# Spatial mixing products for eight feature tiles at once, and earlier operands for two down projections

## The chip, the cores and the metric

The kernel runs on one core of one Trainium2 chip. The metric is device time in microseconds for one execution, the lower the better. Engines are named as in the profile: PE is TensorE (matrix products; PEld its weight loads), DVE is VectorE, ACT is ScalarE, POOL is GpSimd, SP is SyncE, which issues most of the DMA transfers.

## The reference

A two-layer trunk on `x` of 256 frames by 2048 features, all float32. Each sub-layer is `x <- LayerNorm(ALPHA * x + sublayer(x))`. Layer 0 mixes tokens with a gated spatial MLP, layer 1 with latent attention; each is followed by a gated MLP ("ffn") with a causal convolution of width 3. What the change touches is the spatial MLP and both ffn:

```python
def gmlp_mixer(x, w_in, ln_g, ln_b, w_s, b_s, w_out):
    z = jax.nn.gelu(x @ w_in)                 # 2048 -> 2 * 6144
    u, v = jnp.split(z, 2, axis=-1)
    v = layer_norm(v, ln_g, ln_b)
    v = v.reshape(B, S // 128, 128, 8, 768)   # windows of 128 frames, 8 groups of features
    w = w_s * mask[None]                      # 8 x 128 x 128
    s = jnp.einsum('gij,bnjgd->bnigd', w, v) + jnp.transpose(b_s)[None, None, :, :, None]
    return (u * s.reshape(B, S, 6144)) @ w_out

def conv_ffn(x, w_up, conv_w, conv_b, w_down):
    h = x @ w_up                              # 2048 -> 2 * 5504
    h = conv(h, conv_w) + conv_b              # width 3, causal, one filter a feature
    a, g = jnp.split(h, 2, axis=-1)
    return (jax.nn.silu(g) * a) @ w_down
```

## The kernel before

Every float32 operand is held as a high and a low part, and a product is made of high x high, low x high and high x low. Weights stream in chunks of 1 MB: `Feed` loads a chunk into one of three raw buffers (SP's queue), ACT casts its high part `wh` (L127), DVE subtracts to get the low part `wl` (L130). Both lie in a pool of 14 large buffers ("big"), which also holds activations and the operands of the down projections. PSUM has 8 banks of 128 x 512 float32, handed out as they come free.

The stages run one after the other. In layer 0: the `v` half of the up projection and its norm; then the `u` half, 12 groups (`gi`) of four feature tiles of 128 features by 256 frames, four weight chunks a group. In a group `prod_a` accumulates the four tiles in four banks: for each pair of chunks 32 products with `wh` (512 wide: the high and the low part of x side by side), then 32 with `wl` (256 wide) or the other way about. Behind the group, `gate` takes each tile F: `sum_halves` adds the bank's two halves (`lo_u` on ACT, L391; `h_u` on DVE, L393), ACT applies Gelu, PE makes two spatial products `s` of 128 x 128 in a bank of its own, DVE makes the bias term `sb` (L796), scales the two windows (`sg`, twice, L801) and multiplies (`pT`, L803). `v` must be normalised for them, which `norm_v` does for slice `gi // 2 + 1` within the even groups.

`down(NF_GM, pT, "wo")` then multiplies `pT` with the output weights, in two passes over pairs of feature tiles ("units") in the order of the table `PLAN`. A unit is "wide" (the three products above), "seven" (a scheme with seven products in place of eight, with sums of operands) or "parked" (the same, with weight sums computed beforehand, stored in DRAM by POOL's DMAs and fetched). Its accumulators stand in two sets of four banks, DIRECT and OWN; the first pass takes banks for DIRECT first. `acts.make` builds the high and low operands of a unit (`wo0wx`, `dn00wx`, `dn01px`: projection, unit, kind); L476 is the cast of a parked unit's turned sums, L479 and L480 the cast and the subtraction of the operand itself. `down` makes three units ahead of use; what is made earlier is done by the loops that feed it.

The ffn of a layer runs 22 groups; group 0 belongs to the boundary of the stages and groups 1 to 21 to its loop. A group is four tiles (two pairs `a`, `g`), each convolved (`conv`: L838 on ACT, L839 and L841 on DVE), then Silu (L855) and the product `act`. After group 19 the loop makes the operands of the first two units, after group 20 those of the third; then `down` follows. Layer 1's attention and its ffn use the same helpers. All products of PE are recorded under one line, L234. Instructions of an engine run in the order in which its queue holds them, which a scheduler decides from the program's order and its model of times; a weight cast of `Feed` can come ahead of an earlier evacuation and the reverse.

Of the kernel before, what the change touches and what calls it, by code (L numbers as in the profile page):

```python
# [8 lines left out]
F32 = mybir.dt.float32  # L9
F32R = mybir.dt.float32r  # L10
BF16 = mybir.dt.bfloat16
AF = mybir.ActivationFunctionType
# [48 lines left out]
        NF_FF: ("0e 1p 2e 3s 4e 5e 6p 7e 8s 9e 10e 11p 12e 13s 14e 15p 16e 17s 18e 19s 20e 21e",  # L61
                "21e 20e 19p 18e 17s 16e 15p 14e 13s 12e 11p 10s 9e 8s 7p 6e 5s 4e 3e 2e 1e 0e")}
KINDS = {"e": "wide", "s": "seven", "p": "parked"}
LEAD = 5
KEEP = {"wide": 4, "seven": 6, "parked": 6}

# [147 lines left out]
def trunk(ctx: ExitStack, tc: tile.TileContext, x, xT, gm_in, gm_wout, ffn_up, ffn_dn,  # L214
# [12 lines left out]
    def slot(shape, name, dt=F32, tag="big"):  # L227
        return big.tile(shape, dt, tag=tag, name=name, bufs=SLOTS[tag])

    def bank(name):  # L230
        return ps.tile([P, 512], F32, tag="bank", name=name)

    def mm(o, l, r, start, stop):
        recent[0] = nc.tensor.matmul(o, l, r, start=start, stop=stop, skip_group_check=True)  # L234
# [250 lines left out]
    def down(n_k, src, tag, ln, acts, skew=SKEW):  # L485

        ln.begin()
        seq = plan(n_k)
        line = seq[0] + seq[1]
        late, at = [], 0  # L490
        fetched = max([i for i, t in enumerate(line) if t[1] == "parked"], default=len(line))
        for hf, units in enumerate(seq):
            n = len(units)
            last = [u for u, kind in units if kind != "wide"][-1]
            acc = Banks(f"{tag}{hf}", OWN + DIRECT if hf else DIRECT + OWN)
            for i, (u, kind) in enumerate(units):
                left = n - 1 - i if hf == 1 else n
                for n2, v2 in enumerate(line[at : at + 3]):
                    acts.make(*v2, "side" if at + n2 > fetched or at + n2 >= len(seq[0]) and v2[1] == "parked" else "big")
                if i == n - 8:  # L500
                    ln.fetch(hf)
                got = feed.next(splits=2 if left > 5 or left == 0 else 3, loads=2 if left > 2 or left == 0 else 1)
                if left == 6:
                    ln.prep()
                a, sums = acts.got[u]
                if left < skew:
                    late.append((a, *got))
                elif kind == "wide":
                    acc.eight(a, *got)
                else:  # L510
                    acc.seven(a, sums, *got, 512 if kind == "parked" else 0)
                    if u == last:
                        for j, t in enumerate(acc.rest()):
                            ln.fold(j // 2, 2 * hf + j % 2, t)
                at += 1
                for v2 in [v2 for v2 in acts.got if not any(v2 == w2 and n2 < KEEP[kind2]
                                                            for n2, (w2, kind2) in enumerate(line[at:]))]:
                    acts.got.pop(v2)
            if hf == 0:
                for j, m in enumerate(DIRECT):  # L520
# [260 lines left out]
    pT = [None] * 6  # L781
    acts = Acts(pT, "wo", NF_GM)

    def gate(F, acc):
        g = F // 6
        sl, pos = F // 8, F % 8
        if pT[sl] is None:
            pT[sl] = slot([P, 8, S], f"pT{sl}", tag="side" if sl else "big")
        h = sum_halves(acc, f"u{F}")
        u = tp.tile([P, S], F32, tag="t1", name=f"u{F}", bufs=T1)  # L790
        nc.scalar.activation(u, h, AF.Gelu_apprx_tanh)
        sp = bank(f"s{F}")
        for b in range(2):
            mm(sp[:, b * P : (b + 1) * P], v[sl][:, b, pos * P : (pos + 1) * P], wTg[:, g, :], True, True)
        t = tp.tile([P, P], F32, tag="sbias", name=f"sb{F}", bufs=1)
        nc.vector.scalar_tensor_tensor(t, rowsum[:, g, :], cst[:, C_GMB + F : C_GMB + F + 1], bsb[:, g, :],  # L796
                                       ALU.mult, ALU.add)
        s = tp.tile([P, S], F32, tag="t1", name=f"sg{F}", bufs=T1)
        for b in range(2):
            c = slice(b * P, (b + 1) * P)  # L800
            nc.vector.scalar_tensor_tensor(s[:, c], sp[:, c], cst[:, C_GMG + F : C_GMG + F + 1], t,  # L801
                                           ALU.mult, ALU.add)
        nc.vector.tensor_tensor(pT[sl][:, pos, :], u, s, ALU.mult)  # L803

    def park_all(until):

# [5 lines left out]
    for gi in range(12):  # L812
        acc = [bank(f"u{gi}_{f}") for f in range(4)]
        for c in range(4):
            hi, lo = feed.next()
            prod_a(acc, xhl, range(4 * c, 4 * c + 4), hi, lo)
            if gi > 0:
                next(jobs, None)
            if gi % 2 == 0 and gi < 10 and c in (1, 2):
                norm_v(gi // 2 + 1, c - 1)  # L820
        if gi == 11:
            for t in plan(NF_GM)[0][:2]:
                acts.make(*t)
        for f in range(4):
            gate(4 * gi + f, acc[f])
        if gi == 10:
            acts.make(*plan(NF_GM)[0][2])

# [16 lines left out]
    def ffn(layer, ln, acc, end, last):  # L845
# [28 lines left out]
        for gi in range(1, 22):  # L874
            nt, nk = (4, 4) if gi < 21 else (2, 8)
            acc = [bank(f"up{layer}_{gi}_{f}") for f in range(nt)]
            for c in range(KD // nk):
                hi, lo = feed.next()
                prod_a(acc, xhl, range(nk * c, nk * c + nk), hi, lo)
                if gi > 1:  # L880
                    next(jobs, None)
                if gi == 1 and c == 0:
                    after(1, 1, None)
                    for f in range(2):
                        pair(f, hb[0][:, f * S : (f + 1) * S], hb[1][:, f * S : (f + 1) * S])
            for f in range(nt // 2):
                pair(2 * gi + f, acc[f], acc[nt // 2 + f])
            if 1 < gi < 6:
                old.restore(gi - 2)
            if gi in (4, 6):  # L890
                old.park(gi // 2 - 2)
            if gi == 19:
                for t in plan(NF_FF)[0][:2]:
                    acts.make(*t)
            if gi == 20:
                acts.make(*plan(NF_FF)[0][2])
        ln = Norm(2 * layer + 1, {}, old.put_away, last)
        return (ln, *down(NF_FF, act, f"dn{layer}", ln, acts, 4 if last else SKEW))

# [372 lines left out]
```

## Time and profile before

| | |
|---|---|
| Median of 3 runs | 2488.39 us (2487.24 to 2489.69) |
| Profiled execution | 2486.63 us, its span 2484.8 us |
| Mean granted PE clock | 0.999 |
| PE busy | 2468.0 us, 99% |
| DVE busy | 1992.9 us, 80% |
| ACT busy | 1424.6 us, 57% |
| DMA | 606.17 MB, mean 244 GB/s |

The span is what the profile covers; the execution's own time is 1.8 us longer. Busy shares are averages over all stages. The u groups lie between about 279 and 545 us of the span, the `wo` projection begins at 545; chunk 2 of the ffn's group 20 (chunk 226 of the whole stream) begins in layer 0 near 1262 us, its fellow in layer 1 near 2230 us.

### The profile page before, as it was taken

The page shows a single profiled execution, that of the slowest core. Times are in us where ns is not written, and L with a number is a line of the kernel's source. Part 1 is how long each engine was busy: PE and PEld are TensorE (multiplying, and loading weights), DVE is VectorE, ACT ScalarE, POOL GpSimd, SP SyncE. Part 2 cuts the span into 40 slices and gives each one's busy share as a digit, 9 for nine tenths or more (in the row PEclk, how much of TensorE's full clock was granted, in tenths as well). Part 3 has the DMA queues.
Part 4 walks back from the last instruction along what each step waited for, and adds up shares of the span by engine and source line. Part 5 has one row for each costly group of instructions (what it writes and reads, how often), then busy time and mean ns, then how long its engine had stood idle before and what let it go on. Part 6 is the DMA issues. An engine that isn't in the chain of part 4 may idle for free. (4 is left out here: it accounts for less than half of the span.)

```text
span 2484.8 us, 33520 instructions
## 1 busy us (share of the span) xinstructions
PE 2468.0 (99%) x12995; PEld 2122.3 (85%) x12995; DVE 1992.9 (80%) x2802; ACT 1424.6 (57%) x1979; POOL 89.0 (4%) x173
## 2 busy tenths in 40 slices
PE   9999999999999999999999999999999999999998
PEld 7888888888888888888888888988888888888886
DVE  7999866679898789787677897856598788768798
ACT  6676544446565756566554566655566656655453
POOL 0000000000000000000000000000001000000000
PEclk9999999999999999999999999999999999999999
DMA  7556544546665689788558885544489789647885
GB/s 280 203 206 223 198 173 169 185 170 214 209 203 203 218 349 351 286 335 315 188 198 319 302 305 185 182 155 151 174 294 347 293 333 341 238 155 286 299 325 199
DMA packets 108991, 606.17 MB, mean 244 GB/s; under 512 B 10272, under 2 KB 11040, under 8 KB 61600
## 3 DMA queue, kind: packets, MB, share of 16 engines
q1 hardware_dynamic: 84832, 463.51, 52.2%
q0 software_dynamic: 24000, 140.52, 14.7%
q8 instruction: 102, 1.67, 0.3%
q14 instruction: 57, 0.47, 0.1%
HBM read 538.98 MB, written 65.01 MB: 243 GB/s over the span
## 5 line engine op out<-in xcount | busy, mean ns | idle before, releaser
L130 DVE TENSOR_TENSOR wl<-raw,wh 128x1024 fp32r<-128x1024 f32 (+4 forms) x693 | 968.2, 1418 | 222.4 <-ACT wh L127 136.9
L127 ACT CAST wh<-raw 128x1024 fp32r<-128x1024 f32 (+4 forms) x693 | 820.2, 1211 | 388.0 <-PE u L234 84.6
L234 PE MATMUL up<-xhl,wh 128*128 128x512 f32 x2624 | 612.0, 390 | 0.9 <-ACT wh L127 0.9
L234 PEld LDWEIGHTS up<-xhl,wh 128*128 128x128 f32 x2624 | 487.3, 188 | 99.4 <-ACT wh L127 1.8
L234 PEld LDWEIGHTS up<-xhl,wl 128*128 128x128 f32 x2624 | 325.9, 192 | 7.2 <-DVE wl L130 0.7
L234 PE MATMUL up<-xhl,wl 128*128 128x256 f32 x2624 | 328.5, 283 | 0.5 <-DVE wl L130 0.5
L234 PE MATMUL u<-xhl,wh 128*128 128x512 f32 x768 | 184.7, 393 | 0.1
L234 PEld LDWEIGHTS u<-xhl,wh 128*128 128x128 f32 x768 | 141.0, 188 | 31.6 <-issue 3.8
L127 ACT CAST th<-ts 128x1536 fp32r<-128x1536 f32 x106 | 110.1, 1052 | 87.8 <-DVE ts L137 62.7
L130 DVE TENSOR_TENSOR tl<-ts,th 128x1536 fp32r<-128x1536 f32 x106 | 125.3, 1218 | 8.1 <-PE dn_p L234 3.4
L234 PEld LDWEIGHTS u<-xhl,wl 128*128 128x128 f32 x768 | 95.4, 192 | 2.0
L234 PE MATMUL u<-xhl,wl 128*128 128x256 f32 x768 | 96.0, 283 | 0.0
L234 PE MATMUL mo<-wh,oT 128*128 128x512 f32 x256 | 83.0, 404 | 0.0
L137 DVE TENSOR_TENSOR ts<-ts,raw 128x512 f32<-128x512 f32 x106 | 72.6, 685 | 0.9
L234 PE MATMUL v_q<-wh,xhl 128*128 128x512 f32 x224 | 69.2, 390 | 1.2 <-ACT wh L127 1.2
L137 DVE TENSOR_TENSOR ts<-raw 128x1024 f32<-128x1024 f32 x53 | 64.5, 1218 | 0.9 <-PE wo_q L234 0.7
L234 PE MATMUL v_p<-wh,xhl 128*128 128x512 f32 x192 | 59.8, 390 | 0.1
L234 PEld LDWEIGHTS mo<-wh,oT 128*128 128x128 f32 x256 | 45.4, 189 | 7.4 <-DVE oT L1109 0.2
L234 PEld LDWEIGHTS v_q<-wh,xhl 128*128 128x128 f32 x224 | 41.9, 188 | 10.7 <-ACT wh L127 2.1
L234 PE MATMUL mo<-wl,oT 128*128 128x512 f32 x128 | 50.2, 392 | 0.0
L686 ACT ACTIVATE lny<-lnt,lncol 128x128 f32<-128x128 f32 x96 | 36.6, 471 | 15.6 <-PE lnt L682 15.5
L171 DVE TENSOR_TENSOR pwl<-praw,pwh 128x1536 fp32r<-128x1536 f32 x16 | 28.1, 1755 | 20.4 <-ACT pwh L170 20.4
(1701 smaller groups left out, 4165.4 us busy)
## 6 DMA issues: line engine op xcount, KB each, us to landing
raw<-in_ffn_up_dram SPq DMA_DIRECT2D x172, 1024.0 KB, 6.4
raw<-in_gm_in_dram SPq DMA_DIRECT2D x93, 1024.0 KB, 4.8
raw<-in_ffn_dn_dram SPq DMA_DIRECT2D x68, 1024.0 KB, 6.8
raw<-in_gm_wout_dram SPq DMA_DIRECT2D x48, 1024.0 KB, 5.4
praw<-in_ffn_dn_dram POOLq DMA_DIRECT2D x16, 1024.0 KB, 14.8
keptth<-pth POOLq DMA_DIRECT2D x16, 1024.0 KB, 6.4
kepttl<-ptl POOLq DMA_DIRECT2D x16, 1024.0 KB, 8.8
fth<-keptth POOLq DMA_DIRECT2D x16, 1024.0 KB, 9.5
```

The source lines that it names most:

```text
L127: cast = self.nc.scalar.copy(hi, raw)
L130: self.nc.vector.tensor_tensor(lo, raw, hi.bitcast(F32), ALU.subtract)
L137: add = lambda o, a, b: self.nc.vector.tensor_tensor(o, a, b, ALU.add)
L171: pin(nc.vector.tensor_tensor(lo[:, 0:cols], raw[:, o : o + cols], hi[:, 0:cols].bitcast(F32), ALU.subtract))
L234: recent[0] = nc.tensor.matmul(o, l, r, start=start, stop=stop, skip_group_check=True)
L686: nc.scalar.activation(y[:, j], t[:, j * P : (j + 1) * P], AF.Identity, bias=lncol[:, o : o + 1], scale=lncol[:, g : g + 1])
```

## The change

The spatial products of eight feature tiles (`v` slice `gi // 2`) are made together after each even group, two tiles to a bank: `s{sl}_{i}`. The scaling writes both windows of a tile at once, directly into `pT`, and the evacuated, Gelu'd tile then multiplies it in place. Odd groups make no spatial products. The evacuations of a group's four tiles (`sum_halves`) stand together ahead of the rest in the code.

In the ffn, operands of unit 0 are made in chunk 1 of group 19, of unit 1 in chunk 0 of group 20, and of unit 2 in chunk 2 of group 20 (`FIRST`), where they were made after groups 19, 19 and 20. In `down`, one condition gets a further term.

```diff
+FIRST = ((19, 1), (20, 0), (20, 2))
...
-                    acts.make(*v2, "side" if at + n2 > fetched or at + n2 >= len(seq[0]) and v2[1] == "parked" else "big")
+                    acts.make(*v2, "side" if at + n2 > fetched or at + n2 >= len(seq[0]) and v2[1] == "parked" and v2[0] < 20 else "big")
...
-    def gate(F, acc):
...
+    def spatial(sl):
+        pT[sl] = slot([P, 8, S], f"pT{sl}", tag="side" if sl else "big")
+        sp = [bank(f"s{sl}_{i}") for i in range(4)]
+        for pos in range(8):
+            for b in range(2):
+                o = (pos % 2) * S + b * P
+                mm(sp[pos // 2][:, o : o + P], v[sl][:, b, pos * P : (pos + 1) * P], wTg[:, (8 * sl + pos) // 6, :],
+                   True, True)
+        return sp
+
+    def scaled(sl, sp):
+        for pos in range(8):
+            F = 8 * sl + pos
+            t = tp.tile([P, P], F32, tag="sbias", name=f"sb{F}", bufs=1)
+            nc.vector.scalar_tensor_tensor(t, rowsum[:, F // 6, :], cst[:, C_GMB + F : C_GMB + F + 1],
+                                           bsb[:, F // 6, :], ALU.mult, ALU.add)
+            nc.vector.scalar_tensor_tensor(pT[sl][:, pos, :].rearrange("p (b c) -> p b c", b=2),
+                                           sp[pos // 2][:, pos % 2 * S : pos % 2 * S + S].rearrange("p (b c) -> p b c", b=2),
+                                           cst[:, C_GMG + F : C_GMG + F + 1], t[:, None, :].to_broadcast([P, 2, P]),
                                            ALU.mult, ALU.add)
...
-        for f in range(4):
-            gate(4 * gi + f, acc[f])
+        if gi % 2 == 0:
+            sp = spatial(gi // 2)
+        hs = [sum_halves(acc[f], f"u{4 * gi + f}") for f in range(4)]
+        for h in hs:
+            nc.scalar.activation(h, h, AF.Gelu_apprx_tanh)
+        if gi % 2 == 0:
+            scaled(gi // 2, sp)
+        for f, h in enumerate(hs):
+            t = pT[gi // 2][:, 4 * (gi % 2) + f, :]
+            nc.vector.tensor_tensor(t, t, h, ALU.mult)
...
                 if gi > 1:
                     next(jobs, None)
+                if (gi, c) in FIRST:
+                    acts.make(*plan(NF_FF)[0][FIRST.index((gi, c))])
...
-            if gi == 19:
-                for t in plan(NF_FF)[0][:2]:
-                    acts.make(*t)
-            if gi == 20:
-                acts.make(*plan(NF_FF)[0][2])
```

How the queues change, at the three places of which the prediction speaks. Line numbers of the changed program are one higher near `sum_halves`, PE's products and the casts, and ten higher near `conv`.

DVE's queue behind group 4 of the u stage, from the evacuation of its first tile (16) on; `u4_0` is the bank of that tile, `s16` the bank of its spatial products. Before:

```order
L393 TENSOR_TENSOR h_u16_3095<-u4_0_2926,lo_u16_3093 128x256
L801 SCALAR_TENSOR_TENSOR sg16_3104<-s16_3099,cst_183,sb16_3102 128x128 x2
L393 TENSOR_TENSOR h_u17_3110<-u4_1_2927,lo_u17_3108 128x256
L803 TENSOR_TENSOR pT2_3092<-u16_3097,sg16_3104 128x256
L796 SCALAR_TENSOR_TENSOR sb17_3117<-rsum_1991,cst_183,wT_1869 128x128
L801 SCALAR_TENSOR_TENSOR sg17_3119<-s17_3114,cst_183,sb17_3117 128x128 x2
L393 TENSOR_TENSOR h_u18_3125<-u4_2_2928,lo_u18_3123 128x256
L803 TENSOR_TENSOR pT2_3092<-u17_3112,sg17_3119 128x256
```

Now, with `s2_0` the bank that holds the spatial products of tiles 16 and 17:

```order
L394 TENSOR_TENSOR h_u16_3059<-u4_0_2870,lo_u16_3057 128x256
L394 TENSOR_TENSOR h_u17_3063<-u4_1_2871,lo_u17_3061 128x256
L802 SCALAR_TENSOR_TENSOR pT2_3036<-s2_0_3037,cst_183,sb16_3077 128x256
L394 TENSOR_TENSOR h_u18_3067<-u4_2_2872,lo_u18_3065 128x256
L800 SCALAR_TENSOR_TENSOR sb17_3080<-rsum_1991,cst_183,wT_1869 128x128
L394 TENSOR_TENSOR h_u19_3071<-u4_3_2873,lo_u19_3069 128x256
L802 SCALAR_TENSOR_TENSOR pT2_3036<-s2_0_3037,cst_183,sb17_3080 128x256
L835 TENSOR_TENSOR pT2_3036<-pT2_3036,h_u16_3059 128x256
```

The evacuations of tiles 16 and 17 stand next to each other, those of 18 and 19 one instruction apart; the two `sg` became one instruction on `pT2`, and the multiplication comes later.

PE's queue from the last products of group 11 to the first of the `wo` projection (`wo0_q3` is an accumulator of its first pass, `wo0wx` its unit 0's operand). Before:

```order
L234 MATMUL u11_2_4516<-xhl0_3_87,wh95_4558 128x512
L234 MATMUL u11_3_4517<-xhl0_3_87,wh95_4558 128x512
L234 MATMUL s44_4685<-wT_1869,v5_1971 128x128 x2
L234 MATMUL s45_4700<-wT_1869,v5_1971 128x128 x2
L234 MATMUL s46_4715<-wT_1869,v5_1971 128x128 x2
L234 MATMUL s47_4730<-wT_1869,v5_1971 128x128 x2
L234 MATMUL wo0_q3_4741<-wh96_4598,wo0wx_4674 128x512 x2
L234 MATMUL wo0_q3_4741<-wl96_4599,wo0wx_4674 128x512
```

Now the same place, and ahead of it PE's rows between groups 10 and 11:

```order
L235 MATMUL u11_1_4383<-xhl0_3_87,wh95_4426 128x512
L235 MATMUL u11_2_4384<-xhl0_3_87,wh95_4426 128x512
L235 MATMUL u11_3_4385<-xhl0_3_87,wh95_4426 128x512
L235 MATMUL wo0_q3_4573<-wh96_4466,wo0wx_4542 128x512 x2
L235 MATMUL wo0_q3_4573<-wl96_4467,wo0wx_4542 128x512
```
```order
L235 MATMUL u10_3_4142<-xhl0_3_87,wh91_4183 128x512
L235 MATMUL s5_0_4304<-wT_1869,v5_1971 128x128 x4
L235 MATMUL s5_1_4305<-wT_1869,v5_1971 128x128 x4
L235 MATMUL s5_2_4306<-wT_1869,v5_1971 128x128 x4
L235 MATMUL s5_3_4307<-wT_1869,v5_1971 128x128 x4
L235 MATMUL u11_0_4382<-xhl0_0_84,wh92_4223 128x512
```

The spatial products of tiles 44 to 47 moved from behind group 11 to behind group 10, where they stand with those of tiles 40 to 43.

ACT's queue in layer 0's ffn, from the weights of group 20 on (`wh224` to `wh227` are its chunks' high parts, `lo_0a38` the first evacuation of group 19). Before:

```order
L127 CAST wh225_10803<-raw225_10729 128x1024 x2
L479 CAST dn00wx_10881<-act0_0_6848 128x2x256 x2
L391 COPY lo_0a38_10843<-up0_19_0_10679 128x256
L479 CAST dn01px_10884<-act0_0_6848 128x512
...
L855 ACTIVATE s0_39_10878<-c_0g39_10874 128x256
L476 CAST dn01px_10884<-dn01pt_10885 128x512
L127 CAST wh226_10898<-raw226_10769 128x1024 x2
L127 CAST wh227_10938<-raw227_10809 128x1024 x2
```

Now:

```order
L128 CAST wh224_10598<-raw224_10521 128x1024 x2
L128 CAST wh225_10638<-raw225_10561 128x1024 x2
L392 COPY lo_0a38_10678<-up0_19_0_10511 128x256
L128 CAST wh226_10720<-raw226_10604 128x1024
L848 ACTIVATE c_0a38_10682<-h_0a38_10680,cst_183 128x256
L392 COPY lo_0g38_10686<-up0_19_2_10513 128x256
L128 CAST wh226_10720<-raw226_10604 128x1024
...
L480 CAST dn01px_10760<-act0_0_6680 128x512
L848 ACTIVATE c_0a39_10701<-h_0a39_10699,cst_183 128x256
L392 COPY lo_0g39_10705<-up0_19_3_10514 128x256
L477 CAST dn01px_10760<-dn01pt_10761 128x512
L128 CAST wh227_10770<-raw227_10644 128x1024
```

The first cast of `wh226` moved ahead of every part of `dn01px`, and `dn00wx` (shown before behind `wh225`) now stands ahead of `wh224`.

More of the change, by code (lines that the diff above doesn't have):

```diff
@@ L782, in trunk @@
     acts = Acts(pT, "wo", NF_GM)
-    def gate(F, acc):
[L785 to L801, printed above, removed]
+    def spatial(sl):
[16 more added lines that the diff above has]
+                                           cst[:, C_GMG + F : C_GMG + F + 1], t[:, None, :].to_broadcast([P, 2, P]),
                                            ALU.mult, ALU.add)
-        nc.vector.tensor_tensor(pT[sl][:, pos, :], u, s, ALU.mult)
     def park_all(until):
```

## The prediction

> **What bounds the kernel now.** I read the page's busy shares first, then what TensorE (PE) waited for over the whole span.
>
> ```profile
> span 2484.8 us, 33520 instructions
> ...
> PE 2468.0 (99%) x12995; PEld 2122.3 (85%) x12995; DVE 1992.9 (80%) x2802; ACT 1424.6 (57%) x1979; POOL 89.0 (4%) x173
> ```
> ```profile
> PE wo_q L234 <- DVE h_u L393: 1.7, 1, 1.7
> ...
> PE up L234 <- ACT wh L127: 0.9, 2, 0.5
> ```
>
> PE is busy 99% of 2484.8 us, and its waits are few and short (us in total, times, longest us). So only two things can move the time: the number of PE products, and those few gaps. The change leaves the products as they are (16 `s` products per group of the u stage become 32 in every second group), so I looked at the gaps in the three places that it touches: the u groups, the start of the `wo` projection, and the end of each ffn up-projection. PE's products are pipelined, and a short wait for a PSUM bank shows in no view of waits; it shows where rows start. Rows of the timeline (start, busy us, engine, line, operation, tiles, count) in the u stage, one usual group boundary and then the boundary of group 10:
>
> ```profile
> 375.64 1.95 PE L234 MATMUL s<-wT,v 128*128 128x128 f32 x16
> 375.84 1.04 ACT L127 CAST wh<-raw 128x1024 fp32r<-128x1024 f32 x1 [0.25 <-PE u L234]
> ...
> 377.11 0.35 ACT L391 COPY lo_u<-u 128x256 f32<-128x256 f32 x1
> 377.35 4.16 PE L234 MATMUL u<-xhl,wh 128*128 128x512 f32 x16
> 377.50 0.42 DVE L393 TENSOR_TENSOR h_u<-u,lo_u 128x256 f32<-128x256 f32 x1 [0.60 <-ACT lo_u L391]
> ...
> 381.34 4.00 PE L234 MATMUL u<-xhl,wl 128*128 128x256 f32 x32
> ```
> ```profile
> 521.44 1.95 PE L234 MATMUL s<-wT,v 128*128 128x128 f32 x16
> 523.14 3.89 PE L234 MATMUL u<-xhl,wh 128*128 128x512 f32 x16
> 526.87 3.40 PE L234 MATMUL u<-xhl,wl 128*128 128x256 f32 x27
> ```
>
> From the first `s` product to the first `wl` product is 381.34 - 375.64 = 5.70 us at the usual boundary and 526.87 - 521.44 = 5.43 us at the last-but-one: 0.27 us more for the same 32 products. In the gap, ACT puts a weight cast (375.84) between the low halves of tiles 0 and 1 (377.11), so `h_u` of tile 1, which frees its bank, ends at 377.50 + 0.42 = 377.92, when the next group has already run a product or two from 377.35. The same shows over nine groups (stretch and length, busy time of PE, PEld, DVE, ACT and POOL, clock, DMA share, GB/s; the third row is a group of the ffn, as long but with no `s` products):
>
> ```profile
> 302.70:521.44 218.74, 218.64 (x1297) 192.55 (x1296) 138.58 (x254) 94.19 (x143) 0.00 (x0) 1.00 0.49 173
> 521.44:545.47 24.03, 24.03 (x145) 21.48 (x144) 18.89 (x35) 13.38 (x18) 0.00 (x0) 1.00 0.40 134
> 2114.39:2136.61 22.22, 22.22 (x130) 19.68 (x129) 19.62 (x32) 15.44 (x25) 0.00 (x0) 1.00 0.74 268
> ```
>
> 218.74 / 9 = 24.30 us a group against 24.03: again 0.27. And 24.03 - 22.22 = 1.81 us is what one place with 16 `s` products costs.
>
> **A, the u boundaries.** Removed: the 16 `s` products after every group. Added: 32 after each even group, for its own four tiles and the four of the next group. On DVE (the rows behind group 4, shown with the change) the evacuations `h_u` now stand nearly together: between two of them is at most one scaling or one bias step, where it was two scalings and two more steps. And each two 128-wide scalings (`sg`) become one 256-wide one written to `pT`. That form is not in the trace; its nearest rows (busy us, mean ns of one, idle before) are
>
> ```profile
> L801 DVE SCALAR_TENSOR_TENSOR sg<-s,cst,sb 128x128 f32<-128x128 f32 x96 | 29.1, 345 | 4.5 <-PE s L234 2.4
> L839 DVE SCALAR_TENSOR_TENSOR c_0g<-h_0g,cst,c_0g 128x255 f32<-128x255 f32 x41 | 19.6, 479 | 7.5 <-ACT c_0g L838 7.5
> ```
>
> It is bounded by one `sg` (345 ns) and two (690 ns); I take 479 ns, since `c_0g` is as wide. That is 0.21 us less for each of 48 tiles, 10 us of DVE, none of it on PE's path by itself. The two kinds of boundary then differ:
> - Even groups. 32 products, at 1.70 us for 16 (521.44 to 523.14), run 3.4 us before the next group asks for the first tile's bank; the others follow one product (3.73 / 16 = 0.23 us) apart. `h_u` of tile 2 now takes the place of tile 1 today, with one cast ahead of it on ACT: 377.92 - 375.64 = 2.28 us behind the first `s` product. Tile 3 follows a bias step (as long as one `sg`, 0.35) later, with its own 0.42: 3.05. It is wanted at 3.4 + 3 x 0.23 = 4.1. Slack 1.05 us.
> - Odd groups. No `s` products; the next group begins on the four banks which the scaled `s` products freed a group earlier.
>
> Nine waits of 0.27 us go: 2.45 us. Bounds: 0 (the wait only moves) and 2.45, and a further 0.7 at most if six places fewer also save their ends: 1.81 - 1.70 = 0.11 each. I take 2.45, since the place with no wait (521.44) has that 0.11 still.
>
> Today's trace has a wait of 0.27 us where a group returns to a bank of the group before it. The Trainium skill ("Perfetto Trace Analysis", Matmuls) wants independent groups of products to rotate through different PSUM banks, so that the evacuation of one overlaps the next; by that rule, which the 0.27 bears out, odd boundaries gain and even ones, which return to the banks just filled, do not, and half of A would be left, 1.2 us.
>
> **B, the start of `wo`.** The four pairs of `s` products between group 11 and the first `wo` product are gone from this place; they stand behind group 10 now. Rows of before:
>
> ```profile
> 543.93 1.28 DVE L480 TENSOR_TENSOR wo0wx<-pT,wo0wx 128x512 fp32r<-128x512 f32 x2
> 545.47 1.95 PE L234 MATMUL s<-wT,v 128*128 128x128 f32 x16
> 547.00 1.75 DVE L130 TENSOR_TENSOR wl<-raw,wh 128x1536 fp32r<-128x1536 f32 x1
> 548.67 0.42 DVE L393 TENSOR_TENSOR h_u<-u,lo_u 128x256 f32<-128x256 f32 x1
> 549.14 0.73 PE L234 MATMUL wo_q<-wh,wo0wx 128*128 128x512 f32 x2 [1.73 <-DVE h_u L393]
> ```
>
> 545.47 to 549.14 is 3.67 us, of which 1.70 are 16 products (as at 521.44) and 1.97 a wait: `wo_q` took the banks of group 11, whose evacuation (548.67) stood behind the next weights' low half (547.00). Now the products of this place are at group 10, and the four banks that they filled are long scaled when group 11 ends, so the first `wo` accumulators go there and nothing waits for `h_u44`. Next late would be the operand `wo0wx`: finished at 543.93 + 1.28 = 545.2, 0.3 us ahead of the end of group 11. Its place in DVE's queue does not change. Bounds 0 and 1.97; I take 1.97. The other accumulators, on group 11's banks, are first used by unit 2, two chunks (2 x 22.22 / 4 = 11 us) later; ahead of the last of the four `h_u` DVE has, by such rows' durations, about 9 us of work (an estimate).
>
> **C, the last ffn groups.** Both layers have a gap in group 20:
>
> ```profile
> 1258.31 3.81 PE L234 MATMUL up<-xhl,wh 128*128 128x512 f32 x16
> 1260.99 0.62 ACT L476 CAST dn01px<-dn01pt 128x512 fp32r<-128x512 f32 x1 [1.29 <-DVE dn01pt L290]
> 1261.51 3.90 ACT L127 CAST wh<-raw 128x1024 fp32r<-128x1024 f32 x4
> 1262.61 3.93 PE L234 MATMUL up<-xhl,wh 128*128 128x512 f32 x16 [0.48 <-ACT wh L127]
> 1266.37 0.88 PE L234 MATMUL up<-xhl,wl 128*128 128x256 f32 x6
> ```
> ```profile
> 2114.39 7.44 PE L234 MATMUL up<-xhl,wh 128*128 128x512 f32 x32
> 2121.67 4.00 PE L234 MATMUL up<-xhl,wl 128*128 128x256 f32 x32
> 2225.52 3.81 PE L234 MATMUL up<-xhl,wh 128*128 128x512 f32 x16
> 2229.80 3.96 PE L234 MATMUL up<-xhl,wh 128*128 128x512 f32 x16 [0.47 <-ACT wh L127]
> 2233.60 2.68 PE L234 MATMUL up<-xhl,wl 128*128 128x256 f32 x21
> ```
>
> Undisturbed, 32 such products take 2121.67 - 2114.39 = 7.28 us, 16 take 3.64. In the two gaps they take 4.30 + 3.76 = 8.06 (1258.31 to 1266.37) and 4.28 + 3.80 = 8.08: 0.78 + 0.80 = 1.58 us lost. Cause: the cast of chunk 226 (1261.51) stands on ACT behind `dn01px`, which itself waits 1.29 us for DVE. The change makes the operands of the down projection's unit 0 in chunk 1 of group 19 and of unit 1 in chunk 0 of group 20, and ACT's rows shown with the change have both casts of `wh226` ahead of `dn01px`. So this gap goes, if chunk 227 has time: its low part is wanted a chunk later, 22.22 / 4 = 5.6 us, which covers `dn01px` and its wait (0.62 + 1.29), a cast (1.04) and the first subtraction (1.22, below): 4.2. Also `dn00wx` takes one of the large buffers about two chunks earlier, which leaves five for weights instead of six. A chunk's low half is two subtractions:
>
> ```profile
> L130 DVE TENSOR_TENSOR wl<-raw,wh 128x1024 fp32r<-128x1024 f32 x516 | 615.2, 1219 | 146.4 <-ACT wh L127 86.3 <-issue 52.0 <-PE u L234 4.1
> ```
>
> These are 2 x 1.22 us of the 5.6 us between a buffer's release and its use, so the tightest keeps about 3 us. Bounds 0 and 1.58; I take 1.58.
>
> The edit in `down` changes nothing: a second-half parked unit is 19, 15, 11 or 7, all below 20.
>
> Queues: SP's and POOL's instructions keep their order. Only POOL's first prefetch, which waits for an `s` product of the last group, starts a group (24 us) sooner, where the DMA engines are busy 0.40 of the time (row 521.44:545.47): nothing, and 1.97 (B) if it should delay the first `wo` weights.
>
> **Sum.** 2.45 + 1.97 + 1.58 = 6.0 us. The profiled execution took 2486.63 us (span 2484.8), 1.76 us under the median 2488.39. So its like would be 2480.6, and the median **2482.4**. About 0.2%, 5.0 us, is what a measurement of this kernel can tell from no change.
>
> **Rivals.**
> - *The `wo` stage is DVE's.* Rows (PE, PEld, DVE, ACT, POOL):
>
> ```profile
> 546.00:560.00 14.00, 12.28 (x61) 10.20 (x60) 13.71 (x27) 8.85 (x13) 0.84 (x1) 1.00 0.62 215
> 560.00:802.00 242.00, 242.00 (x1071) 200.44 (x1070) 217.12 (x246) 138.64 (x134) 0.00 (x0) 1.00 0.65 213
> ```
>
> DVE is busy 13.71 of 14 us after group 11, so PE, starting 3.67 us sooner, may wait for `wl` a little later and give B back: -4.0 us, 2484.4. Against: PE is solid at 242.00 of 242.00 after, and the changed gate saves DVE 0.2 us a tile. 0.13.
> - *The reordering doesn't do what it says in the ffn*: the gap moves from chunk 226 to 227, C is lost: -4.4, 2484.0. For: `dn01px` still waits for DVE. 0.08.
> - *The even boundaries wait*, as by the rule on banks: if another cast (1.04) stands ahead and the scaling takes 0.69 (0.21 more), `h_u` of tile 3 comes 1.25 us later, 0.2 over its slack, six times: -4.8, 2483.6. It would be slower than before only from (6.0 + 5.0) / 6 = 1.8 us over the slack. 0.06.
> - *Slower: buffers in groups 19 and 20.* Unit 0's operand holds a large buffer for longer, and the casts behind it wait. It decides when more than the 3 us of slack stands ahead of a weight's cast; then up to a chunk, 5.6 us, is lost in each layer, 11.1 in both, and C does not come: -4.4 + 11.1 = +6.7, 2495.1. For: these are the groups in which the gaps are today. Against: each of those is under 1 us, and it takes more. 0.11.
>
> **How the numbers follow.** Forecast 0.62. Low end: all of A, B, C and the 0.7 of A's upper bound, less 1.2 us, about what the three runs lie from their median (2487.24 to 2489.69): 2480.5. High end: B and C both given back (-2.4) and 1.2 of spread: 2487.2; only the slower case lies outside. Faster is the forecast alone, 0.62; within 0.2% are the first three rivals, 0.27; slower 0.11.
>
> **What would show it.** In the changed profile: no `s` products after odd groups; from the first `s` product to the first `wl` of the next group 5.43 + 1.70 = 7.1 us at even groups; two groups in 2 x 24.03 = 48.1 us instead of 48.6; `wo_q` directly behind group 11 with no wait for `h_u`; 7.3 us from the first to the second half of chunk 226's pair in both layers. Wrong would be: a PE wait for `wl` or `wo0wx` past 545 us, a new PE wait for `wh` near group 20, or groups that still take 24.3 us.

## The result, and the profile after

The changed kernel takes 2482.0 us (median of 18 runs, 2480.79 to 2487.51), the kernel before, run beside it, 2487.0 us (18 runs, 2484.47 to 2492.37): 5.0 us less by the medians. The ratio is 0.9982, with a 95% interval of 0.9976 to 0.9989, that is 2.7 to 6.0 us less.

The page of the changed kernel's profiled execution (own time 2482.76 us, 3.87 less than that of before):

```profile
span 2480.9 us, 33450 instructions
...
PE 2464.9 (99%) x12995; PEld 2123.1 (86%) x12995; DVE 1986.6 (80%) x2754; ACT 1421.8 (57%) x1979; POOL 89.0 (4%) x173
```

What PE waited for (us in total, times, longest):

```profile
PE up L235 <- DVE wl L131: 2.0, 4, 0.7
PE v_p L235 <- ACT wh L128: 1.6, 1, 1.6
PE warm L235 <- POOL idle L281: 1.3, 1, 1.3
PE v_q L235 <- ACT wh L128: 0.3, 1, 0.3
```

The wait for `h_u` at the start of `wo` and the two of `up` for `wh` are gone. New is the first row: four waits of the ffn for low halves of weights, 2.0 us where it was 0.5.

The three places, as timelines of PE and DVE. An even boundary of the u stage:

```profile
374.95 3.73 PE L235 MATMUL s<-wT,v 128*128 128x128 f32 x32
378.44 3.89 PE L235 MATMUL u<-xhl,wh 128*128 128x512 f32 x16
382.16 4.00 PE L235 MATMUL u<-xhl,wl 128*128 128x256 f32 x32
...
376.55 0.42 DVE L394 TENSOR_TENSOR h_u<-u,lo_u 128x256 f32<-128x256 f32 x1
376.89 0.34 DVE L800 SCALAR_TENSOR_TENSOR sb<-rsum,cst,wT 128x128 f32<-128x128 f32 x1
377.15 0.42 DVE L394 TENSOR_TENSOR h_u<-u,lo_u 128x256 f32<-128x256 f32 x1
```

The last evacuation ends at 377.57, 2.6 us behind the first `s` product (the forecast had 3.05), and the next group begins at 378.44. Its 16 products take 382.16 - 378.44 = 3.72 us; 381.34 - 377.35 = 3.99 before. From the first `s` to the first `wl` product it is 7.21 us (7.1 forecast). The start of `wo`:

```profile
541.23 3.82 PE L235 MATMUL u<-xhl,wh 128*128 128x512 f32 x16
544.88 0.62 PE L235 MATMUL wo_q<-wh,wo0wx 128*128 128x512 f32 x2
```

`wo` begins 3.65 us behind the start of the last 16 u products, which is what these take. Chunk 226 in both layers' ffn:

```profile
1253.90 7.44 PE L235 MATMUL up<-xhl,wh 128*128 128x512 f32 x32
1261.18 4.00 PE L235 MATMUL up<-xhl,wl 128*128 128x256 f32 x32
```
```profile
2222.45 7.44 PE L235 MATMUL up<-xhl,wh 128*128 128x512 f32 x32
2229.74 4.00 PE L235 MATMUL up<-xhl,wl 128*128 128x256 f32 x32
```

32 products in 7.28 and 7.29 us, no gap. And the place of the new waits, in the first half of layer 1's ffn:

```profile
1984.96 1.22 PE L235 MATMUL up<-xhl,wl 128*128 128x256 f32 x8 [0.68 <-DVE wl L131]
1986.69 1.21 PE L235 MATMUL up<-xhl,wl 128*128 128x256 f32 x8 [0.52 <-DVE wl L131]
```

For the accounts, each trace is cut where PE's first product of a stage starts (the first `u`, the first `wo` product, the first product of ffn group 1, the first product of its down projection); the lengths are differences of those starts. "u" runs from the first u product to the first `wo` product, "ffn 0" and "ffn 1" from group 1 to the down projection. The last column compares the runs with the kernel before, each time with runs of it made beside them. The rows come from several sessions and chips, in which the median of the kernel before lay between 2485.49 and 2487.02 us, so versions are compared by the ratio and not by the median.

| profile | u | ffn 0 | ffn 1 | median us (runs) | ratio, 95% interval |
|---|---|---|---|---|---|
| before | 293.19 | 462.27 | 463.21 | 2487.02 (18) | 1 |
| changed | 288.68 | 461.52 | 464.50 | 2482.00 (18) | 0.9982, 0.9976 to 0.9989 |
| gate_only | 288.68 | 463.40 | 462.59 | 2483.03 (11) | 0.9990, 0.9982 to 0.9999 |
| first_only | 291.37 | 461.49 | 463.03 | 2485.34 (11) | 0.9997, 0.9988 to 1.0006 |
| evac_first | 291.68 | 462.64 | 462.60 | 2486.86 (11) | 1.0005, 0.9996 to 1.0014 |
| last_pair | 291.29 | 462.25 | 468.96 | 2485.56 (11) | 1.0000, 0.9991 to 1.0009 |
| eight_interleaved | 288.68 | 461.49 | 464.13 | 2481.29 (11) | 0.9984, 0.9975 to 0.9993 |
| unit0_only | 288.68 | 461.74 | 464.71 | 2481.87 (8) | 0.9987, 0.9977 to 0.9997 |
| unit1_only | 288.68 | 461.49 | 468.22 | 2481.16 (8) | 0.9980, 0.9970 to 0.9990 |
| changed_again | 288.68 | 461.49 | 461.93 | 2481.01 (9) | 0.9977, 0.9967 to 0.9986 |
| before_again | 291.54 | 463.67 | 464.83 | 2485.64 (8) | 1.0001, 0.9991 to 1.0012 |
| adds_pool | 288.68 | 469.52 | 472.69 | 2500.64 (5) | 1.0055, 1.0043 to 1.0068 |
| spread | 288.67 | 461.54 | 461.46 | 2479.90 (11) | 0.9979, 0.9970 to 0.9988 |
| before_spread | 291.40 | 462.26 | 462.23 | 2484.70 (11) | 0.9997, 0.9988 to 1.0006 |

Between the first two profiles the u stage lost 4.51 us, the `wo` stage 0.19, ffn 0 lost 0.75, ffn 1 grew by 1.29, and 0.31 more came at the start and in the attention: -3.85 of a span that fell by 3.9.

### The profile page after: what moved, and what is told of

Same layout as the page of the kernel before. It is cut to its first block, busy times and chain, and to the rows that moved or that the text cites. A ratio compares the mean times of both kernels' runs of the same rounds, so it can differ in the third digit from the quotient of the medians.

```text
span 2480.9 us, 33450 instructions
## 1 busy us (share of the span) xinstructions
PE 2464.9 (99%) x12995; PEld 2123.1 (86%) x12995; DVE 1986.6 (80%) x2754; ACT 1421.8 (57%) x1979; POOL 89.0 (4%) x173
## 5 line engine op out<-in xcount | busy, mean ns | idle before, releaser
L131 DVE TENSOR_TENSOR tl<-ts,th 128x1536 fp32r<-128x1536 f32 x106 | 125.4, 1219 | 8.0 <-PE dn_p L235 3.4
L138 DVE TENSOR_TENSOR ts<-raw 128x1024 f32<-128x1024 f32 x53 | 64.6, 1219 | 1.2 <-PE wo_q L235 1.0
```

The source lines that it names most:

```text
L131: self.nc.vector.tensor_tensor(lo, raw, hi.bitcast(F32), ALU.subtract)
L138: add = lambda o, a, b: self.nc.vector.tensor_tensor(o, a, b, ALU.add)
```

## The experiments

**Which half of the change does what.** `gate_only` takes the ffn part out again, `first_only` makes it alone.

```diff
 gate_only, against the changed kernel
-                if (gi, c) in FIRST:
-                    acts.make(*plan(NF_FF)[0][FIRST.index((gi, c))])
+            if gi == 19: (units 0 and 1, as before)
+            if gi == 20: (unit 2, as before)
 first_only, against the kernel before: the same lines the other way about
```

> The change without its ffn part: the operands of the three down units are made after groups 19 and 20 again. Theory (the gain is a sum of separate waits): groups of the u stage 24.03 us, the first wo product directly behind group 11, so 4.4 us less than before; the two gaps of about 0.8 us at chunk 226 of each layer's ffn are back. 2482.6 where before is 2487.0. Rival (the whole gain comes from the u stage, the ffn part does nothing): 5.0 to 6.0 us less, as the full change, and no gap at chunk 226. The waits for wl in layer 1's ffn, 2.65 us in the changed profile and 0.68 in the one before: if they are an accident of an execution, any value from 0 to 3 us here; if they come from the earlier operands in the ffn, 0.68 or less.

> The kernel before with the ffn part of the change alone. Theory: the gaps at chunk 226 go in both layers, 1.6 us less than before; the u groups keep 24.30 us and wo its wait of 1.97. Rival (the edit only moves the wait to chunk 227): no change, and a gap of about 0.8 us a chunk later. Layer 1's waits for wl: if they come from this edit, about 2.6 us of them and the time is that of before or longer.

`gate_only`: the u stage is 288.68 us, as in the full change to the hundredth, and the gap at chunk 226 is back:

```profile
1254.49 3.81 PE L235 MATMUL up<-xhl,wh 128*128 128x512 f32 x16
1258.78 3.93 PE L235 MATMUL up<-xhl,wh 128*128 128x512 f32 x16 [0.48 <-ACT wh L128]
```

`first_only`: no gap there, ffn 0 at 461.49. So C belongs to the ffn part and A and B to the gate, as forecast. The times of these two (0.9990 and 0.9997 of before) are too near each other's intervals to size them; the stages are not. By the medians (before beside them: 2485.71) gate_only gained 2.7 us, not the 4.4 that I expected, and first_only 0.4, not 1.6. In gate_only ffn 0 also took longer than the gap explains (463.40 us against 462.27 in before): three weights came late there, near 1019, 1053 and 1087 us. A surprise is in `first_only`: nine waits of 0.27 us stand in its u stage, but the stage is 1.82 us shorter than before. Its list of waits has none at the start of `wo`, though nothing was changed there.

**What B hung on.** `last_pair` moves only group 11's spatial products; `before_again` is the kernel before in another execution.

```diff
 last_pair, against the kernel before
-        for f in range(4):
-            gate(4 * gi + f, acc[f])
+        if gi < 10: (as before)
+        else: (spatial(5) behind group 10, evacuation, scaled(5), product, as in the change)
```

> The kernel before, with the new form (eight tiles at once, gated in place) for the last two groups alone: the spatial products of group 11 move behind group 10. Theory B (the wait of 1.97 us at the start of wo is one for group 11's banks, which the products behind it forced): it goes, wo begins 3.4 us earlier after the end of group 11 and the whole is about 2.0 us shorter. Rival (DVE's work bounds the start of wo): PE waits for the low half of a weight or for the operand within the next 15 us and gets nothing.

> The kernel before once more, for another profile. Theory: nine waits of 0.27 us at the u boundaries and both gaps at chunk 226 (0.8 us) stand as in the first profile, since they come from the order of instructions; the wait at the start of wo is not fixed, since its chain begins at the landing of the load for chunk 97: wo begins 9.43 us behind that landing or right behind PE, whichever is later, so 0 to 2 us. Rival: 1.9 us again whatever the landing.

`last_pair` has no wait at `wo` (u stage 1.90 us shorter than in before, 0.25 shorter than in before_again) and no gain in time (ratio 1.0000). Its profile lost more in ffn 1 (468.96), but that is one run of eleven. In the kernels that keep the old place of the products, the wait is another one each time. Rows of ACT's cast of chunk 97 and of the first `wo` product in before, first_only, evac_first and before_spread:

```profile
539.78 1.91 ACT L127 CAST wh<-raw 128x2048 fp32r<-128x2048 f32 x1 [5.18 <-DMA raw<-in_gm_wout_dram]
549.14 0.73 PE L234 MATMUL wo_q<-wh,wo0wx 128*128 128x512 f32 x2 [1.73 <-DVE h_u L393]
```
```profile
539.12 1.91 ACT L128 CAST wh<-raw 128x2048 fp32r<-128x2048 f32 x1 [3.42 <-DMA raw<-in_gm_wout_dram]
548.47 0.73 PE L235 MATMUL wo_q<-wh,wo0wx 128*128 128x512 f32 x2
```
```profile
539.90 1.90 ACT L127 CAST wh<-raw 128x2048 fp32r<-128x2048 f32 x1 [3.86 <-DMA raw<-in_gm_wout_dram]
549.25 0.73 PE L234 MATMUL wo_q<-wh,wo0wx 128*128 128x512 f32 x2 [0.75 <-DVE h_u L393]
```
```profile
538.31 1.90 ACT L127 CAST wh<-raw 128x2048 fp32r<-128x2048 f32 x1 [3.40 <-DMA raw<-in_gm_wout_dram]
547.65 0.73 PE L236 MATMUL wo_q<-wh,wo0wx 128*128 128x512 f32 x2
```

549.14 - 539.78 = 9.36, then 9.35, 9.35 and 9.34. In `before_again` it is 547.49 - 538.14 = 9.35. In all five the cast starts 0.07 to 0.08 us behind the landing of its load. So in the old order the start of `wo` is tied to the cast of chunk 97, which starts when its load lands: cast, low half, operand, the sums of chunk 98, and `h_u44` behind all of them. From the first of the 16 `s` products to `wo_q`, less their 1.70 us, the wait was 1.97 us in the first profile, where that load took 7.1 us; 1.00 in evac_first (549.25 - 546.55) with a load of 5.7, 0.34 in before_again (547.49 - 545.45) with one of 5.5, 0.18 in first_only and 0.16 in before_spread with 5.3 each. In the changed kernel `wo` starts 544.88 - 536.57 = 8.31 us behind this cast, sooner than the old chain allows, and right behind group 11. The mechanism of B was the forecast's; its 1.97 us was one execution's draw, and the largest of the five. That fits what last_pair and gate_only gained, which is less than I expected.

**What removes the waits of the u stage.** `evac_first` puts the four evacuations ahead and keeps 16 products a group; `eight_interleaved` keeps 32 products and puts the gating back between the evacuations.

```diff
 evac_first, against the kernel before
...
+        hs = [sum_halves(acc[f], f"u{4 * gi + f}") for f in range(4)]
         for f in range(4):
-            gate(4 * gi + f, acc[f])
+            gate(4 * gi + f, hs[f])
 eight_interleaved, against the changed kernel
...
-        hs = [sum_halves(acc[f], f"u{4 * gi + f}") for f in range(4)]
+        for f in range(4):
+            h = sum_halves(acc[f], f"u{4 * gi + f}")
...
+            if gi % 2 == 0:
+                scaled(gi // 2, sp, (2 * f, 2 * f + 2))
```

> The kernel before with one edit: the four evacuations of a group stand ahead of the gating of its first tile. The spatial products stay 16 a group, and all operations of DVE stay as they were. Theory A1 (the 0.27 us at a group's start is the evacuation of tile 1 behind a weight cast on ACT, so order alone cures it): groups of 24.03 us, 2.4 us less by the u stage. Theory A2 (the longer cover of 32 products or the lighter DVE work is what cures it): groups keep 24.30 us, no gain. The wait at the start of wo stays either way, between 1.2 and 2.0 us.

> The changed kernel, but each tile is evacuated, passed through Gelu and multiplied in turn, as in the kernel before, with two scalings between; eight tiles' spatial products at once stay. Theory A (what removes the wait at the u boundaries is 3.4 us of products ahead of the bank's next use): no bank wait, or one of at most 0.2 us at the last tile of even groups; the stretch from the first u product to wo stays 288.7 us, at most 1.2 more. Rival (the order of the evacuations does it): 0.2 to 0.3 us at every boundary, 291 us.

My expectation A1 fell. In `evac_first` tile 1 is in time, but the last tile is not. PE, and the last `lo_u` and `h_u` of the group:

```profile
377.00 1.95 PE L234 MATMUL s<-wT,v 128*128 128x128 f32 x16
378.71 4.11 PE L234 MATMUL u<-xhl,wh 128*128 128x512 f32 x16
382.65 0.52 PE L234 MATMUL u<-xhl,wl 128*128 128x256 f32 x3
...
378.42 1.05 ACT L127 CAST wh<-raw 128x1024 fp32r<-128x1024 f32 x1
379.37 0.38 ACT L391 COPY lo_u<-u 128x256 f32<-128x256 f32 x1
...
379.77 0.42 DVE L393 TENSOR_TENSOR h_u<-u,lo_u 128x256 f32<-128x256 f32 x1 [0.80 <-ACT lo_u L391]
```

The 16 products take 382.65 - 378.71 = 3.94 us, 0.21 over 3.73: a second cast (378.42) stands ahead of tile 3's low half, and `h_u` ends at 380.19, 1.5 us after the group has begun. With 1.7 us of cover (the time that the spatial products take between two groups) the order alone hands the wait from tile 1 to tile 3. `eight_interleaved`, with the old order and 3.5 us of cover, has none: 288.68 us again. So it is the 32 products at once that pay, and the regrouping of the evacuations in the code adds nothing to it. Both versions with 32 products also have the lighter scaling, and no run takes that out alone; but two `sg` back to back took 0.61 us in before (376.29) where the one instruction takes 0.48, and one scaling, 0.13 us longer, ahead of an evacuation that ends 0.87 us before the next group begins (377.57, 378.44) would not make PE wait (an estimate from these rows). One thing does not fit the forecast's sum: the last evacuation of `eight_interleaved` ends at 379.40, 4.34 us behind the first `s` product (375.06), where by that sum it was wanted at 4.1, and PE still does not wait. So the next group did not need tile 3's bank for its first four products; whether it took another bank or came to that tile later, the rows do not show.

**Which part of the ffn edit.** `unit1_only` moves the operand of unit 1 alone, `unit0_only` that of unit 0 alone.

```diff
 unit1_only
-                if (gi, c) in FIRST:
+                if (gi, c) == (20, 0): (unit 1; units 0 and 2 after groups 19 and 20)
 unit0_only
-                if (gi, c) in FIRST:
+                if (gi, c) == (19, 1): (unit 0; units 1 and 2 after groups 19 and 20)
```

> The changed kernel with one part of the ffn edit: the operand of unit 1 (dn01px) is made in chunk 0 of group 20, while those of units 0 and 2 are made after groups 19 and 20 as before. Theory C (the cast of chunk 226 stood behind dn01px): no gap at chunk 226 in either layer, as in the full change. Rival (the earlier unit 0 is what helps): the gaps of about 0.8 us are back.

> The changed kernel with the other part of the ffn edit: the operand of unit 0 is made in chunk 1 of group 19, those of units 1 and 2 after groups 19 and 20 as before. Theory C: dn01px stands ahead of the cast of chunk 226 as before, so the gaps of about 0.8 us are there in both layers. Rival (earlier unit 0 or fewer operations at the end of group 19 is what helps): no gaps.

`unit1_only` has no gap (ffn 0 461.49). But `unit0_only` has nearly none either: 1254.05 to 1261.53 is 7.48 us where it was 8.06 (7.47 in layer 1). ACT there:

```profile
1256.12 0.62 ACT L477 CAST dn01px<-dn01pt 128x512 fp32r<-128x512 f32 x1 [0.69 <-DVE dn01pt L291]
1256.64 3.90 ACT L128 CAST wh<-raw 128x1024 fp32r<-128x1024 f32 x4
```
```profile
1254.05 7.64 PE L235 MATMUL up<-xhl,wh 128*128 128x512 f32 x32
1261.53 4.00 PE L235 MATMUL up<-xhl,wl 128*128 128x256 f32 x32
```

`dn01px` waits 0.69 us for DVE in place of 1.29, because unit 0's subtraction (`dn00wx`, 0.68 us) no longer stands on DVE ahead of it. The cause was right, the cast of chunk 226 behind a wait of `dn01px`; there are two ways to shorten it, and expecting the whole gap back in `unit0_only` was wrong.

**Where the layer-1 waits come from.** `changed_again` is the changed kernel once more. `adds_pool` moves the four sums of a parked unit from DVE to GpSimd. `spread` spreads a unit's preparation over eight chunks where it was six (each `yield` hands back to the loop until the next chunk); `before_spread` does the same in the kernel before.

```diff
 adds_pool
-        add = lambda o, a, b: pin(nc.vector.tensor_tensor(o, a, b, ALU.add))
+        add = lambda o, a, b: pin(nc.gpsimd.tensor_tensor(o, a, b, ALU.add))
 spread, before_spread
                 add(r[1], r[1], r[0])
                 add(r[0], r[0], r[2])
+                yield
                 add(r[2], r[2], r[1])
                 add(r[3], r[3], r[2])
                 yield
+                yield
```

> The changed kernel once more, for another profile of the same program. Theory (the layer-1 waits for low halves of weights come from how fast that execution's transfers happened to land): the u stage takes 288.68 us from its first product to the first wo product, to within 0.05, and both ffn are free of the gap at chunk 226; but the stretch from the first ffn product of layer 1 to its down projection differs from the 464.50 us of the first profile by over 0.5 us. Rival (the change itself causes these waits): 464.5 again within 0.2, with the same four waits.

> The changed kernel, but the four sums that prepare each parked unit's weights (praw<-praw, 0.69 us each on DVE) are made on GpSimd. If the late weights of layer 1's ffn come from DVE's queue, where these sums stand ahead of the casts: the waits for low halves go there, 1 to 3 us less than the changed kernel, and less spread between runs. If they come from transfers that land late: no difference. Slower is possible if GpSimd's sums hold up DVE or the parked transfers in its own queue: then DVE's operations beside them take longer than 1.22 us a half, and PE waits more than 2.65 us there.

> The changed kernel, but the preparation of each parked unit is spread over eight weight chunks instead of six: its four sums stand in two chunks, and one more chunk passes before the next step. Theory (layer 1's late weights come where transfers of parked weights and their sums on DVE fall on the same groups): fewer and shorter waits for low halves in the first half of both ffn, layer 1's stretch from its first product to its down projection near the 461.5 us of layer 0, so 0 to 3 us less than the changed kernel and less spread. Rival (the later parts collide with the operands of the down projection in groups 19 and 20, or the buffers are held longer): new waits of PE in the second half of the ffn, slower than the changed kernel.

> The kernel before with the same spreading of the parked units as in the last experiment but one. With the uncertain part of layer 1 out of both, it shows the change alone. Theory (A 2.45, C 1.58 and B between 0 and 1.97 are what the change removes, and layer 1's late weights have nothing to do with it): both ffn stretches as in the spread version plus 0.8 us each, u stage with nine waits of 0.27; the time 4.0 to 6.0 us above the spread version's 2479.9, that is 2483.9 to 2485.9. Rival (the spreading gains only in the changed kernel, because that one feeds layer 1 differently): no better than the kernel before, 2486, with waits for low halves in layer 1.

`changed_again`: the same program, u 288.68 and ffn 0 461.49, but ffn 1 461.93 against 464.50. Its waits of PE in full:

```profile
PE warm L235 <- POOL idle L281: 1.3, 1, 1.3
PE up L235 <- DVE wl L131: 0.2, 1, 0.2
PE v_q L235 <- ACT wh L128: 0.2, 1, 0.2
```

So these waits are not a property of the change. (The two profiles may come from different chips; but eight_interleaved, on the chip of changed_again and with the same queues in this stage, has 464.13.) Over the profiles above, those of adds_pool and of the spread versions left out, ffn 1 is anything from 461.9 to 469.0 us. At the place of the first one, DVE's rows in changed_again and in the changed kernel:

```profile
1981.43 1.22 DVE L131 TENSOR_TENSOR wl<-raw,wh 128x1024 fp32r<-128x1024 f32 x1
1982.57 0.69 DVE L155 TENSOR_TENSOR praw<-praw 128x512 f32<-128x512 f32 x1
1983.17 2.35 DVE L131 TENSOR_TENSOR wl<-raw,wh 128x1024 fp32r<-128x1024 f32 x2
```
```profile
1983.08 0.69 DVE L155 TENSOR_TENSOR praw<-praw 128x512 f32<-128x512 f32 x1
1983.68 1.22 DVE L131 TENSOR_TENSOR wl<-raw,wh 128x1024 fp32r<-128x1024 f32 x1
1984.82 0.69 DVE L155 TENSOR_TENSOR praw<-praw 128x512 f32<-128x512 f32 x1
```

The same queue runs 2.25 us later (1981.43 to 1983.68), and PE, which is only 0.2 us later there, waits. The lag grew in the 200 us before. From 1760 to 2030 us of the span ACT waited 27.0 us for landing weights in the changed kernel and 22.4 in changed_again (47.7 and 40.0 with the parked weights and the residual); up to 1981 us, ahead of the first wait, it was 18.7 and 14.2:

```profile
ACT wh L128 <- DMA raw<-in_ffn_up_dram: 27.0, 11, 5.5
```
```profile
ACT wh L128 <- DMA raw<-in_ffn_up_dram: 22.4, 8, 4.4
```

In `spread` it is 13.0 us (34.2 in all), and PE's whole list of waits is short:

```profile
ACT wh L128 <- DMA raw<-in_ffn_up_dram: 13.0, 10, 3.1
```
```profile
PE warm L237 <- POOL idle L283: 1.3, 1, 1.3
PE v_p L237 <- ACT wh L128: 0.6, 1, 0.6
```

PE waits for no weight of either ffn, and ffn 1 is 461.46 us. The eleven runs lie within 1.8 us of each other (2479.47 to 2481.24), the nine of changed_again within 2.5, the eighteen of the changed kernel within 6.7. The median, 2479.9 us, is the lowest here; but as a ratio it is 0.9979 of before (0.9970 to 0.9988), and the changed kernel has 0.9982 and 0.9977. So a gain in time from the spreading is not shown; shown is a profile without these waits, and no long execution among the eleven. `before_spread` has the clean ffn 1 too, 462.23, of which 0.8 is the gap at chunk 226; its time, 0.9997 of before, cannot be told from no gain either. With the random part out of both profiles, the change is 2484.7 - 2479.9 = 4.8 us by the medians. By the rows of the table it is 2.73 in the u stage, 0.72 and 0.77 in the two ffn, together 4.22.

`adds_pool` was no cure: 1.0055 of before, both ffn 8 us longer. The sums take 1687 ns on GpSimd on average, the next cast of the parked weights waits for them, and some of DVE's subtractions become slower beside them:

```profile
L155 POOL TENSOR_TENSOR praw<-praw 128x512 f32<-128x512 f32 x64 | 108.0, 1687 | 4.2
L171 ACT CAST pth<-praw 128x2048 fp32r<-128x2048 f32 x16 | 30.5, 1909 | 30.6 <-POOL praw L155 30.6
L131 DVE TENSOR_TENSOR wl<-raw,wh 128x1024 fp32r<-128x1024 f32 x516 | 638.7, 1263 | 157.5 <-ACT wh L128 94.1 <-issue 53.1 <-PE up L235 6.5
```

1263 ns is the mean of 516; in the changed kernel it is 1219. The mean hides how: 494 of them take the usual 1.22 us, and 22 take 1.97 to 2.33. Each of the 22 began while an addition ran on GpSimd and ended 1.08 to 1.09 us after that addition's end, as if it had been held up until then. One pair of rows:

```profile
1049.02 1.37 POOL L155 TENSOR_TENSOR praw<-praw 128x512 f32<-128x512 f32 x1
1049.15 2.32 DVE L131 TENSOR_TENSOR wl<-raw,wh 128x1024 fp32r<-128x1024 f32 x1
```

The addition ends at 1050.39, the subtraction at 1051.47. The Trainium skill ("Perfetto Trace Analysis", Optimizing Scalar/DVE Operations) warns that GpSimd and DVE share a read port of SBUF, so that moving work between them might not help; the trace agrees, with these 22 subtractions and 1263 against 1219 ns in the mean. Since this version made DVE's queue lighter and other queues heavier, it doesn't tell how much of the lag is transfers and how much the sums on DVE; `spread` changes both at once. That split stays open. That the lag begins with weights landing late rests on the ACT rows above, not on an experiment that changed transfers alone.

## Why the forecast held, point by point

- **The bound.** PE at 99%, and only its gaps counting, held: DVE lost 6.3 us of work in the whole and nothing came of it but what PE no longer waited for. (The forecast had 10 us: it took two `sg` as 690 ns, and back to back they took 0.61 us.)
- **A, 2.45 us.** Held. The u stage fell by 4.51 us where A and B of that profile made 4.42, and no wait is left at any boundary. The trace of before bears the cause out: PE's load for the third product of the group waits for a semaphore that DVE raises at 377.93, as `h_u` of tile 1 ends. One part of the working was not needed, the order of the evacuations (`eight_interleaved`). The slack of 1.05 us at even groups was enough; the rival in which they wait did not come. By the rule of the Trainium skill on rotating banks ("Perfetto Trace Analysis", Matmuls), as the forecast read it, half of A would have been left. The trace does not bear that out: behind 3.5 us of other products no boundary waits. The 256-wide scaling, taken at 479 ns:

```profile
L802 DVE SCALAR_TENSOR_TENSOR pT<-s,cst,sb 128x256 f32<-128x256 f32 x48 | 22.9, 478 | 1.7 <-PE s L235 1.4
```

- **B, 1.97 us.** The mechanism held, the size did not carry over: the five profiles of the old order show 0.16 to 1.97 us of it, 0.34 in the middle, and their common 9.35 us show why. This is the term that was mis-sized. I read one profile's wait as a constant although the row of its cast said `5.18 <-DMA`, that is, the chain began at a landing. A bound from 0 stood in the text; the middle of the bounds would have been nearer. The rival that DVE's work at the start of `wo` gives B back did not come: PE waits there for nothing.
- **C, 1.58 us.** Held: 0.75 of 0.78 in ffn 0, and in layer 1 the 32 products that took 8.08 us take 7.29. That the edit only moves the wait to chunk 227 is out, and so is the case in which the earlier operand starves the weights of a buffer: the casts of group 20 in the changed profile wait for PE or not at all.
- **The sum.** -6.0 forecast, -5.0 measured, 2482.4 against 2482.0 for the time. That the time agreed within 0.4 us is luck: the gain was forecast 1.0 us too large, and the median from which it was taken was 1.4 too high (2488.39 of 3 runs, 2487.02 of 18). What was not in the sum is that ffn 1 differs between executions of one program, by 2.6 us in the two profiles of the changed kernel and by 1.6 in those of before, which is as much as A or C and hides either in single runs.

## What to carry to other kernels

Before a gap is booked as a gain, see what its chain starts from: gaps that come from the order of a queue (A, C) were the same in every profile, to a few hundredths; one whose chain starts at a landing transfer (B, and by the rows above the waits of ffn 1) is a draw, and one profile shows only one draw. The bank wait here was cured by enough other products ahead of the reuse, not by tidying the evacuations, which handed it to the last tile. And where side work (here the parked units) runs in bursts beside a loop with little slack, try spreading it over the room that the loop has: with two more `yield`s the changed kernel's profile shows no late weight in either ffn, though the medians do not show a gain clear of noise.

## What the runs showed of the hardware that I had not expected

From issue to landing, loads of 1 MB from one queue took between 4.6 and 12.3 us in layer 1's ffn, and the same load in two executions of one program differed by up to 1.9 us (8.6 and 10.5 us for one of them), while the instructions of DVE and ACT kept their times to 0.02 us. One addition of 128 x 512 float32 took 1687 ns on average on GpSimd (1.28 to 1.48 us in 42 of the 64) against 685 on DVE. It cost most of DVE's subtractions nothing, and 0.75 to 1.1 us each of the 22 that were held up by one: by their ends, the two instructions took turns (spans on GpSimd are rough).
